# A transformer trunk in split float32: stationary tiles in low SBUF, four seven-product chunks, an accumulating DMA for half of a split

## The chip, the cores and the metric

One core of one Trainium2 chip runs the whole program in one launch. The time is device microseconds of that core. Three runs of the kernel before gave a median of 2034.09 us (2033.9 to 2034.6).

## The reference, cut to what matters

Four layers; each adds half a feed-forward block (FFN), then one attention (differential, block, sparse, differential), then half a second FFN. Inputs, outputs and weights are float32, with 256 tokens of width 1024 and a hidden width of 2816.

```
def swiglu(x, w_in, w_out):
    gate, up = jnp.split(x @ w_in, 2, axis=-1)
    return (jax.nn.silu(gate) * up) @ w_out

for i in range(DEPTH):
    g = norm_g[i]
    h = h + 0.5 * rms_norm(swiglu(rms_norm(h, g[0]), ffn_w_in[i, 0], ffn_w_out[i, 0]), g[1])
    h = h + rms_norm(attention_i(rms_norm(h, g[2])), g[3])
    h = h + 0.5 * rms_norm(swiglu(rms_norm(h, g[4]), ffn_w_in[i, 1], ffn_w_out[i, 1]), g[5])
```

So there are eight FFNs and four attentions. The change touches the FFNs, and in the attentions only the place of some tiles.

## The kernel before, in words

**Split products.** TensorE multiplies in the type fp32r. For float32 accuracy each operand is held as two fp32r tiles, `hi` (a cast) and `lo` (the value less `hi`), and each product is three matmuls: stationary `xh` with moving `hi`, `xh` with `lo`, `xl` with `hi` (`product`, L139 to 151). A matmul has a 128x128 stationary tile (activations, transposed) and a 128x512 moving tile (weights). The activations' tiles are `xh`/`xl` (normed input), `gh`/`gl` (the gated hidden values, transposed in `turn`, L428), `oh`/`ol` (attention output), and `sh`/`sl_` (sums of activations, `sums`, L266).

**Weights.** Weights arrive in blocks of 1 MB as `raw` tiles, loaded by DMAs that SP issues. For each block ACT writes `hi` (`hilo`, L154) and DVE writes `lo` (L155). Four such pairs (UNITS) may be alive; the pool `wt` holds them. Seven raw tiles (RAWS) may be alive. `plan_plain`, `plan_out` and `plan_wino` list the loads and the splits in order, and `fill` (L400) issues them as places come free. A place comes free when TensorE has read a pair for the last time (`close`).

**One FFN.** The hidden width is cut into five chunks of 512 columns (j = 0 to 4) and one of 256. A chunk makes gate and up for two token tiles (t = 0, 1) of 128 tokens. In a plain chunk these are 8 half products (2 token tiles, gate and up, 2 halves of the width 1024) of 12 matmuls each. In a Winograd chunk (`wino`, L465; j = 2 and 4) they are seven such products, named after their weights: `b00`, `t1`, `b10`, `t3`, `t2`, `b11`, `t4`. The weights t1 to t4 are sums of quarters of the weight block, which DVE adds in the raw tiles (L376); the activations' sums are `sh`/`sl_`. The seven results are put together from four PSUM tiles (`pa` to `pd`) with copies on ACT (L483, L488) and adds on DVE (L478). Between these products the chunk also carries the second half of the chunk before it: two transposes (`turn`, PSUM tile `tpg`) and four output steps `o(t, k)` (`out_steps`, L234), each 12 matmuls into the `y` banks with the second weights. Those arrive as two blocks `ko0` and `ko1`.

**Order.** The Tile framework schedules instructions on each engine from the program and its pools' dependencies; so the order on an engine is not that of the code. Pools also set the addresses: a pool is laid out after the one before it. Before, the order in SBUF is `const`, `raw`, `wt`, `xp`, then the work tiles and the pools of the phase. In KiB of each partition: `hi` at 50 to 82, `lo` at 82 to 114, `xh`/`xl` at 114 to 130, `oh`/`ol` at 169 to 185, `sh`/`sl_` at 193 to 209, `gh`/`gl` at 209 to 217.

**The FFN's end** (L554 to 567): after the last chunk's products come its transposes and the last output steps; `turn(last, 1)` stands after `out(last - 1, 1, ...)`.

Of the kernel before, what the change touches and what calls it, by code (L numbers as in the profile page):

```python
# [9 lines left out]
F32 = mybir.dt.float32  # L10
# [6 lines left out]
P = 128  # L17
# [19 lines left out]

RAWS = 7
UNITS = 4
WINO = (2, 4)  # L40

# [5 lines left out]
class Trunk:  # L47
# [217 lines left out]

    def sums(self, X, pool, name):  # L266


        v = self.nc.vector
        half = [[X[t][2][:, b * 512:b * 512 + 512] for b in range(2)] for t in range(NT)]  # L270
        (a00, a01), (a10, a11) = half
        v.tensor_tensor(a11, a11, a10, op=ALU.subtract)
        v.tensor_tensor(a10, a00, a10, op=ALU.subtract)
        v.scalar_tensor_tensor(a00, a11, -1.0, a00, op0=ALU.mult, op1=ALU.subtract)
        v.scalar_tensor_tensor(a01, a01, -1.0, a00, op0=ALU.mult, op1=ALU.subtract)
        out = []
        for t in range(NT):
            sh = pool.tile([P, KD, P], F32R, tag="sh", name=f"sh{name}_{t}")
            sl = pool.tile([P, KD, P], F32R, tag="sl_", name=f"sl_{name}_{t}")
            src = X[t][2].rearrange("p (k n) -> p k n", n=P)  # L280
            self.hilo(src, sh, sl)
            out.append((sh, sl))
        return out

    def ffn(self, l, f, X, ahead, end):
        nc = self.nc
        with self.tc.tile_pool(name=f"ffn{l}{f}", bufs=2, reuse_waits="tile") as pool:
# [36 lines left out]

            def split(n, of, done=False):
# [6 lines left out]
                for k in range(0, nk, m):  # L332
                    self.hilo(v[:, k:k + m], hi[:, k:k + m], lo[:, k:k + m])
                if done:
                    free(of)
                U[n] = hi, lo, nk, w
# [4 lines left out]

            def plan(n, src):
                loads.append(lambda: raw(n, src))
                preps.append((None, lambda: split(n, n, True)))

# [9 lines left out]
            def plan_out(j):  # L355
                c0, w = chunks[j]
                for k in range(0, w // P, 2):
                    plan((j, "o", k), (w_out, c0 + k * P, 2, 0, D))

            def plan_wino(j):  # L360


                c0, w = chunks[j]
                name = lambda n: (j, n)
                quarter = lambda k, u: (w_in, k * 512, 4, u * D_FF + c0, w)
                ko = [(j - 1, "o", k) for k in (0, 2)]
                c1 = chunks[j - 1][0]
                osrc = [(w_out, c1 + k * P, 2, 0, D) for k in (0, 2)]
                for n, src in ((name("b00"), quarter(0, 0)), (name("b01"), quarter(0, 1)),
                               (name("b10"), quarter(1, 0)), (ko[0], osrc[0]), (name("b11"), quarter(1, 1)),  # L370
                               (ko[1], osrc[1])):
                    loads.append(lambda n=n, src=src: raw(n, src))

                def add(to, b):
                    to, b = R[name(to)], R[name(b)]
                    nc.vector.tensor_tensor(to, to, b, op=ALU.add)  # L376

                def t1():
                    add("b00", "b01")
                    split(name("t1"), name("b00"))  # L380

                def t3():
                    add("b01", "b11")
                    split(name("t3"), name("b01"), True)

                def t2():
                    add("b00", "b11")
                    split(name("t2"), name("b00"))

                def t4():  # L390
                    split(name("t4"), name("b00"), True)
                    free(name("b10"))

                mine = [lambda: split(name("b00"), name("b00")), t1, lambda: split(name("b10"), name("b10")),
                        lambda: split(ko[0], ko[0], True), t3, t2]
                mine += [lambda: (add("b00", "b10"), split(name("b11"), name("b11"), True)),
                         lambda: split(ko[1], ko[1], True), t4]
                preps.extend((None, f) for f in mine)

            def fill():  # L400
                while loads and live["raw"] < RAWS:
                    loads.pop(0)()
                while preps and live["unit"] < UNITS:
                    preps.pop(0)[1]()
                    while loads and live["raw"] < RAWS:
                        loads.pop(0)()
# [20 lines left out]
            def turn(j, t):  # L427
# [3 lines left out]
                for k in range(n):  # L431
                    nc.tensor.transpose(tp[:, k, :], g[:, k * P:(k + 1) * P], self.ident)  # L432
                gh = pool.tile([P, 4, P], F32R, tag="gh", name=f"gh{l}{f}_{j}_{t}")
                gl = pool.tile([P, 4, P], F32R, tag="gl", name=f"gl{l}{f}_{j}_{t}")
                self.hilo(tp[:, :n], gh[:, :n], gl[:, :n])
# [30 lines left out]
            def wino(j):  # L466
# [9 lines left out]

                two = lambda name: pool.tile([P, 512], F32, tag=name, name=f"{name}{l}{f}_{j}", bufs=1)
                add = lambda d, x, z: nc.vector.tensor_tensor(d, x, z, op=ALU.add)  # L478
                s24, s31 = SUMS
                p1, p5, u2 = two("p1"), two("p5"), two("u2")  # L480
                A = bank("pa")
                times(A, X[0][0], 0, "b00", True, True)
                nc.scalar.copy(p1, A)  # L483
                fill()
                turn(j - 1, 0)
                B = bank("pb")
                times(B, s31, 4, "t1", True, True)
                nc.scalar.copy(p5, B)  # L488
                fill()
                turn(j - 1, 1)  # L490
                times(A, X[0][0], 4, "b10", False, True)
                sl0 = gate(0, A, 512, j)
# [4 lines left out]
                fill()  # L497
                o(1, 0)
                E = bank("pd")
                times(E, s24, 0, "t2", True, True)  # L500
                add(u2, E, p1)
                add(p5, p5, u2)
                g1 = pool.tile([P, 512], F32, tag="g", name=f"g{l}{f}_{j}_1")
                add(g1, C, p5)
                fill()
                times(B, s24, 4, "b11", False, True)
                g0 = pool.tile([P, 512], F32, tag="g", name=f"g{l}{f}_{j}_0")
                add(g0, B, u2)
                up(0, g0, 512, sl0, j, nr[0], g0)
                fill()  # L510
                o(0, 2)
                times(C, X[1][0], 4, "t4", False, True)
                sl1 = pool.tile([P, 512], F32, tag="sl", name=f"sl{l}{f}_{j}_1")
                add(sl1, C, u2)
                nc.scalar.activation(sl1, sl1, AF.Silu, scale=X[1][1])
# [18 lines left out]
            def early():  # L534
                SUMS.extend(self.sums(X, pool, f"{l}{f}"))
                for t in range(NT):
# [39 lines left out]
    def attention(self, l, _, X, ahead, end):  # L576
        kind, j = l % 3, l // 3
        with self.tc.tile_pool(name=f"attn{l}", bufs=2, reuse_waits="tile") as pool:
# [4 lines left out]
            for t in range(NT):  # L583
                oh = pool.tile([P, KD, P], F32R, name=f"oh{l}_{t}", bufs=1)
                ol = pool.tile([P, KD, P], F32R, name=f"ol{l}_{t}", bufs=1)
                self.oT.append((oh, ol))
# [739 lines left out]
```

## Time and profile before

| What | Value |
|---|---|
| Median of three runs | 2034.09 us |
| The profiled execution's own time | 2035.73 us |
| Its span, first to last instruction | 2034.0 us |
| Mean granted TensorE clock in it (1.0 is full speed) | 0.998 |
| DVE busy | 1575.7 us (77%) |
| ACT busy | 1150.3 us (57%) |
| POOL busy | 135.0 us (7%) |
| Moved by DMA | 363.15 MB, mean 179 GB/s |

The profile is of one execution, 1.6 us longer than the median. The time outside the span is 1.7 us. Busy times of engines overlap, and a matmul's own duration (some 390 ns) overlaps that of the next, so the pace of TensorE is read from the starts of its matmuls, not from their durations. The same holds on ACT and DVE, where an instruction starts a little before the one before it ends.

### The profile page before, as it was taken

How to read it: one execution, taken by the hardware profiler on the slowest of the kernel's cores; microseconds unless marked ns; L12 is line 12 of the kernel's file. 1: busy time of each engine (PE TensorE's matmuls, PEld its weight loads, DVE VectorE, ACT ScalarE, POOL GpSimd, SP SyncE). 2: the span in 40 equal slices, each digit the busy share in tenths (PEclk: the TensorE clock that was granted, in tenths of full speed). 3: DMA queues.
4: the chain of work that ended last, by engine and by line, in shares of the span. 5: the costliest groups of instructions: out<-in, count | busy, mean ns of one | idle time of the engine just before them, and what ended most of it. 6: DMA issues, size and time to landing. Idle time of an engine off the chain costs nothing.

```text
span 2034.0 us, 25675 instructions
## 1 busy us (share of the span) xinstructions
PE 1987.8 (98%) x9904; PEld 1627.4 (80%) x9904; DVE 1575.7 (77%) x2047; ACT 1150.3 (57%) x1581; POOL 135.0 (7%) x239
## 2 busy tenths in 40 slices
PE   8999999999999999999999998999999999999998
PEld 6888777888888878788888877678887888777887
DVE  6877768877888767788787788868777977767875
ACT  6555566555555566455554565755456555566553
POOL 0000210000000110000000032000000000210000
PEclk9999999999999999999999999999999999999999
DMA  9534637544763553663655475145547534537531
GB/s 352 208 134 149 206 104 270 196 135 164 248 226 106 174 179 138 234 223 108 238 176 207 157 178 166 49 176 176 207 151 263 198 133 149 206 104 260 201 130 62
DMA packets 168651, 363.15 MB, mean 179 GB/s; under 512 B 7760, under 2 KB 36688, under 8 KB 168528
## 3 DMA queue, kind: packets, MB, share of 16 engines
q1 hardware_dynamic: 168528, 361.51, 51.7%
q8 instruction: 78, 1.28, 0.3%
q14 instruction: 45, 0.37, 0.1%
HBM read 360.43 MB, written 1.05 MB: 178 GB/s over the span
## 4 chain that ended last, share of the span: by engine, by line
PE 88%; DVE 6%; ACT 3%; issue 2%; POOL 1%; DMA 0%; SPq 0%; POOLq 0%; DVEq 0%; ACTq 0%
PE ps L150 29%; PE y L245 9%; PE y L247 9%; PE y L246 9%; PE pb L150 4%; PE pc L150 4%; PE pa L150 4%; PE pw L665 4%; PE pw L666 4%; PE pw L667 4%; PE pd L150 2%; DVE lo L155 2%; PE tpg L432 2%; PE sc L739 1%; PE tpp L764 1%
## 5 line engine op out<-in xcount | busy, mean ns | idle before, releaser
L155 DVE TENSOR_TENSOR lo<-raw,hi 128x2048 fp32r<-128x2048 f32 (+3 forms) x458 | 875.4, 1924 | 265.3 <-ACT hi L154 264.8
L154 ACT CAST hi<-raw 128x2048 fp32r<-128x2048 f32 (+3 forms) x458 | 731.6, 1609 | 529.6 <-PE ps L150 157.7
L150 PE MATMUL ps<-hi,xh 128*128 128x512 f32 (+1 forms) x1024 | 378.5, 370 | 4.2 <-ACT xh L154 2.4
L150 PE MATMUL ps<-lo,xh 128*128 128x512 f32 (+1 forms) x1024 | 373.8, 365 | 3.9 <-DVE lo L155 2.2
L150 PE MATMUL ps<-hi,xl 128*128 128x512 f32 (+1 forms) x1024 | 372.9, 365 | 0.6 <-DVE st L202 0.6
L245 PE MATMUL y<-hi,gh 128*128 128x512 f32 x704 | 279.5, 397 | 9.5 <-ACT gh L154 9.5
L246 PE MATMUL y<-lo,gh 128*128 128x512 f32 x704 | 277.7, 394 | 0.0
L247 PE MATMUL y<-hi,gl 128*128 128x512 f32 x704 | 277.3, 395 | 0.0
L150 PEld LDWEIGHTS ps<-lo,xh 128*128 128x128 f32 x1024 | 194.5, 190 | 36.0 <-DVE lo L155 6.0
L150 PEld LDWEIGHTS ps<-hi,xh 128*128 128x128 f32 x1024 | 194.3, 190 | 36.1 <-ACT xh L154 4.4
L150 PEld LDWEIGHTS ps<-hi,xl 128*128 128x128 f32 x1024 | 194.2, 190 | 32.7 <-DVE st L202 1.4
L245 PEld LDWEIGHTS y<-hi,gh 128*128 128x128 f32 x704 | 132.6, 188 | 41.8 <-ACT gh L154 13.0
L665 PE MATMUL pw<-hi,xh 128*128 128x512 f32 (+2 forms) x432 | 165.6, 383 | 0.0
L247 PEld LDWEIGHTS y<-hi,gl 128*128 128x128 f32 x704 | 132.6, 188 | 33.0 <-DVE gl L155 2.2
L117 POOL TENSOR_TENSOR st<-st,negh 128x1 f32<-128x1 f32 (+1 forms) x56 | 46.1, 824 | 1682.3 <-DVE st L204 1610.9
L666 PE MATMUL pw<-lo,xh 128*128 128x512 f32 (+2 forms) x432 | 156.7, 363 | 0.0
L667 PE MATMUL pw<-hi,xl 128*128 128x512 f32 (+2 forms) x432 | 156.3, 362 | 0.0
L246 PEld LDWEIGHTS y<-lo,gh 128*128 128x128 f32 x704 | 132.7, 188 | 29.4
L376 DVE TENSOR_TENSOR raw<-raw,raw 128x2048 f32<-128x2048 f32 x64 | 146.4, 2287 | 1.1
L665 PEld LDWEIGHTS pw<-hi,xh 128*128 128x128 f32 x432 | 82.1, 190 | 19.2 <-issue 7.7
L155 DVE TENSOR_TENSOR gl<-tpg,gh 128x512 fp32r<-128x512 f32 (+1 forms) x96 | 61.6, 641 | 45.5 <-ACT gh L154 45.5
L750 ACT ACTIVATE e<-e,st 128x128 f32<-128x128 f32 (+1 forms) x160 | 71.8, 451 | 40.5 <-DVE st L747 39.8
(214 smaller groups left out, 2751.8 us busy)
## 6 DMA issues: line engine op xcount, KB each, us to landing
raw<-in_ffn_w_in SPq DMA_DIRECT2D x172, 1024.0 KB, 5.3
raw<-in_ffn_w_out SPq DMA_DIRECT2D x88, 1024.0 KB, 4.9
raw<-in_diff_w_in SPq DMA_DIRECT2D x24, 1024.0 KB, 5.2
raw<-in_moba_w_in SPq DMA_DIRECT2D x12, 1024.0 KB, 5.4
raw<-in_nsa_w_in SPq DMA_DIRECT2D x9, 1024.0 KB, 5.1
raw<-in_diff_w_out SPq DMA_DIRECT2D x8, 1024.0 KB, 4.8
gpre<-in_norm_g SPq DMA_DIRECT2D x12, 512.0 KB, 6.3
gpost<-in_norm_g SPq DMA_DIRECT2D x12, 512.0 KB, 7.9
```

The lines of the kernel that those rows point to most:

```text
L117: self.nc.gpsimd.tensor_tensor(r, v, src, op=ALU.pow)
L150: nc.tensor.matmul(out, l, r, start=first and i == 0, stop=last and i == len(steps) - 1, skip_group_check=more)
L154: self.nc.scalar.copy(hi, src)
L155: self.nc.vector.tensor_tensor(lo, src, hi.bitcast(F32), op=ALU.subtract)
L245: nc.tensor.matmul(y[b], x[0][:, kt, :], hi[:, k, s], start=f, stop=False)
L246: nc.tensor.matmul(y[b], x[0][:, kt, :], lo[:, k, s], start=False, stop=False)
L247: nc.tensor.matmul(y[b], x[1][:, kt, :], hi[:, k, s], start=False, stop=l)
L376: nc.vector.tensor_tensor(to, to, b, op=ALU.add)
L665: nc.tensor.matmul(out, x[0][:, kt, :], hi[:, k, :], start=first and i == 0, stop=False)
L666: nc.tensor.matmul(out, x[0][:, kt, :], lo[:, k, :], start=False, stop=False)
L667: nc.tensor.matmul(out, x[1][:, kt, :], hi[:, k, :], start=False, stop=last and i == len(todo) - 1)
L750: nc.scalar.activation(e[:, c, :], e[:, c, :], AF.Exp, scale=-1.0, bias=top[:, c:c + 1], accum_out=tot[:, c:c + 1])
```

## The change

1. The pools' order: `wt` and `xp` first, then a new pool `st` (four tiles, for `sh`/`sl_` and for the attention's `oh`/`ol`), a new pool `gt` (`gh`/`gl`, three of each), then `raw`, `const` and the rest. In KiB: `hi` 4 to 36, `lo` 36 to 68, `xh`/`xl` 68 to 84, `st` 84 to 100, `gt` 100 to 112. The scratch for DMAs whose descriptors POOL makes goes from 16384 to 4096 bytes.
2. Four Winograd chunks (j = 1 to 4) in place of two, and eight raw tiles in place of seven, with `t2` in a tile of its own.
3. For `ko0` and `ko1` of those chunks ACT casts `hi`; ACT then writes the negated value, rounded in the same way, into `lo`; a DMA issued by POOL adds the raw value onto it in SBUF, which leaves `lo` = raw less `hi`. DVE has no part in it. The raw tile and `lo` are both bound to that DMA until it has landed.
4. The products come in the order b00, b10, t2, t1, t3, b11, t4. One PSUM tile `pb` gathers b00, t2, t1 and b11 in turn and is copied out between them, so that three adds on DVE replace five.
5. `turn(last, 1)` moves ahead of `ahead()` at the FFN's end.

The diff, cut to its core:

```diff
-RAWS = 7
+RAWS = 8
 UNITS = 4
-WINO = (2, 4)
+WINO = (1, 2, 3, 4)
...
-        self.const = pool("const", 1)
-        self.raw = pool("raw", 3)
         self.wt = pool("wt", UNITS)
         self.xp = pool("xp", 2)
+        self.st = pool("st", 4)
+        self.gt = pool("gt", 3)
+        self.raw = pool("raw", 3)
+        self.const = pool("const", 1)
...
-            sh = pool.tile([P, KD, P], F32R, tag="sh", name=f"sh{name}_{t}")
-            sl = pool.tile([P, KD, P], F32R, tag="sl_", name=f"sl_{name}_{t}")
+            sh, sl = [self.st.tile([P, KD, P], F32R, tag="s", name=f"s{b}{name}_{t}") for b in "hl"]
...
+                if by_dma:
+                    nc.scalar.copy(hi, v)
+                    nc.scalar.activation(lo, v, AF.Copy, scale=-1.0)
+                    nc.gpsimd.dma_start(lo, v.bitcast(F32R), accum_op=ALU.add)
+                else:
+                    for k in range(0, nk, m):
+                        self.hilo(v[:, k:k + m], hi[:, k:k + m], lo[:, k:k + m])
...
+                preps.extend([
+                    lambda: quarters("b00", [("b00", "b00", "b01")]),
+                    lambda: split(ko[0], ko[0], True, True),
+                    lambda: quarters("b10", [("b01", "b01", "b11"), ("t2", "b00", "b11")]),
+                    lambda: split(name("t2"), name("t2")),
+                    lambda: last_of("t1", "b00"),
+                    lambda: last_of("t3", "b01"),
+                    lambda: split(ko[1], ko[1], True, True),
+                    lambda: last_of("b11", "b11"),
+                    lambda: last_of("t4", "t2", ("t2", "t2", "b10"), "b10")])
...
+                B = bank("pb")
+                times(B, X[0][0], 0, "b00", True, True)
+                sl0 = tile("sl", 0)
+                nc.scalar.copy(sl0, B)
                 fill()
                 turn(j - 1, 0)
+                A = bank("pa")
+                times(A, X[0][0], 4, "b10", True, True)
+                add(sl0, A)
+                nc.scalar.activation(sl0, sl0, AF.Silu, scale=X[0][1])
                 fill()
                 turn(j - 1, 1)
+                times(B, s24, 0, "t2", False, True)
+                sl1 = tile("sl", 1)
+                nc.scalar.copy(sl1, B)
                 fill()
                 o(0, 0)
+                times(B, s31, 4, "t1", False, True)
+                g1 = tile("g", 1)
+                nc.scalar.copy(g1, B)
+                fill()
+                o(1, 0)
                 C = bank("pc")
                 times(C, s31, 0, "t3", True, True)
+                add(g1, C)
                 fill()
                 times(B, s24, 4, "b11", False, True)
+                up(0, B, 512, sl0, j, nr[0])
                 fill()
                 o(0, 2)
                 times(C, X[1][0], 4, "t4", False, True)
+                add(sl1, C)
...
             turn(last, 0)
+            turn(last, 1)
             ahead()
...
-            turn(last, 1)
             turn_x()
...
+    nc = bacc.Bacc("TRN2", target_bir_lowering=False, num_devices=1,
+                   dynamic_dma_scratch_size=4096)
```

In the rows that follow, a row gives the line, the operation, and out<-in by the programs' names with their numbers, as the scheduler ordered them. A tile `hi451` is the unit 451; names of a chunk end in FFN, chunk and token tile (`gh01_2_0`: layer 0, second FFN, chunk 2, tile 0).

**ACT, before:** chunk 2 (Winograd) of the second FFN, from the silu of tile 0. The casts are of b11 (419), ko1 (422), t4 (424) and the two blocks after them.

```order
L418 ACTIVATE sl01_2_0_3322<-pa414_3252,st348_2754 128x512
L154 CAST hi419_3325<-raw398_3038 128x2048
L154 CAST hi422_3356<-raw402_3107 128x2048
L154 CAST hi424_3374<-raw382_2873 128x2048
L154 CAST hi428_3399<-raw404_3113 128x2048
L154 CAST hi430_3420<-raw413_3247 128x2048
```

**ACT, after the change:** the same place of chunk 3 of that FFN, from the cast of t3 (447). Units: ko1 449, b11 451, t4 453, the next chunk's b00 457 and ko0 458.

```order
L156 CAST hi447_3558<-raw426_3310 128x2048
L335 ACTIVATE lo449_3588<-raw435_3420 128x2048
L500 COPY sl01_3_1_3585<-pb443_3513 128x512
L334 CAST hi449_3587<-raw435_3420 128x2048
L156 CAST hi451_3620<-raw429_3340 128x2048
L505 COPY g01_3_1_3618<-pb443_3513 128x512
L156 CAST hi453_3638<-raw433_3402 128x2048
L156 CAST hi457_3660<-raw436_3422 128x2048
L334 CAST hi458_3679<-raw440_3462 128x2048
L335 ACTIVATE lo458_3680<-raw440_3462 128x2048
```

Each Winograd chunk has two more writes of 2048 columns on ACT (L335), and the negated one stands ahead of the cast of `hi` for ko1.

**DVE, after the change:** the start of chunk 3 of the second FFN: `lo` of b10 (441), the sum for t2, `gl` of both token tiles around the first add, `lo` of t2 (442). The tile raw433 lies where ko0's raw tile lay.

```order
L157 TENSOR_TENSOR lo441_3492<-raw431_3370,hi441_3491 128x2048
L381 TENSOR_TENSOR raw433_3402<-raw417_3200,raw429_3340 128x2048
L157 TENSOR_TENSOR gl01_2_0_3540<-tpg01_2_0_3534,gh01_2_0_3539 128x512
L484 TENSOR_TENSOR sl01_3_0_3526<-pa446_3543,sl01_3_0_3526 128x512
L157 TENSOR_TENSOR gl01_2_1_3570<-tpg01_2_1_3564,gh01_2_1_3569 128x512
L157 TENSOR_TENSOR lo442_3510<-raw433_3402,hi442_3509 128x2048
```

The sum for t2 writes a tile that the accumulating DMA of ko0 reads, and both `gl` stand behind it.

**PE, after the change:** the same chunk, where b11 (451, into pb443) meets the first output steps with ko1 (449).

```order
L152 MATMUL pb443_3513<-hi451_3620,sh01_0_3016 128x512
L247 MATMUL y411_0_0_3146<-hi449_3587,gh01_2_0_3539 128x512
L248 MATMUL y411_0_0_3146<-lo449_3588,gh01_2_0_3539 128x512
L249 MATMUL y411_0_0_3146<-hi449_3587,gl01_2_0_3540 128x512
L247 MATMUL y411_0_1_3147<-hi449_3587,gh01_2_0_3539 128x512
L248 MATMUL y411_0_1_3147<-lo449_3588,gh01_2_0_3539 128x512
L152 MATMUL pb443_3513<-lo451_3621,sh01_0_3016 128x512
```

Five output matmuls stand inside b11's product; the second of them reads the `lo` that the DMA of ko1 completes, and the rest of b11 stands behind it.

## Rows read from the trace of the kernel before

**Rows 1.** The page, busy time of each engine

```profile
PE 1987.8 (98%) x9904; PEld 1627.4 (80%) x9904; DVE 1575.7 (77%) x2047; ACT 1150.3 (57%) x1581; POOL 135.0 (7%) x239
```

**Rows 2.** The page, chain that ended last, share by engine

```profile
PE 88%; DVE 6%; ACT 3%; issue 2%; POOL 1%; DMA 0%; SPq 0%; POOLq 0%; DVEq 0%; ACTq 0%
```

**Rows 3.** Windows: chunks 2, 3, 4, second FFN; busy PE, PEld, DVE, ACT, POOL, clock, DMA, GB/s

```profile
375.13:406.54 31.41, 31.41 (x142) 25.62 (x141) 27.61 (x19) 19.71 (x14) 0.00 (x0) 1.00 0.72 249
406.54:440.45 33.91, 33.91 (x154) 27.85 (x153) 23.48 (x15) 14.42 (x11) 0.00 (x0) 1.00 0.42 142
440.45:471.86 31.41, 31.41 (x143) 25.62 (x142) 27.59 (x19) 19.71 (x14) 0.00 (x0) 1.00 0.39 134
```

**Rows 4.** The chain of waits in chunk 2: start us, us, what

```profile
375.13 2.73 PE pa L150 x12
...
381.09 0.44 PE tpg L432 x4
...
387.10 2.79 PE pc L150 x12
...
395.46 2.79 PE pb L150 x12
398.26 0.23 PE y L245
...
403.82 2.72 PE pc L150 x12
```

**Rows 5.** Groups of instructions by form, whole span: busy us, mean ns, idle before

```profile
L155 DVE TENSOR_TENSOR lo<-raw,hi 128x2048 fp32r<-128x2048 f32 x308 | 703.0, 2289 | 217.8 <-ACT hi L154 217.7
L376 DVE TENSOR_TENSOR raw<-raw,raw 128x2048 f32<-128x2048 f32 x64 | 146.4, 2287 | 1.1
L245 PE MATMUL y<-hi,gh 128*128 128x512 f32 x704 | 279.5, 397 | 9.5 <-ACT gh L154 9.5
L245 PE MATMUL y<-hi,oh 128*128 128x512 f32 x128 | 52.5, 410 | 0.0
L150 PE MATMUL pb<-hi,sh 128*128 128x512 f32 x128 | 51.8, 405 | 0.0
L150 PE MATMUL pd<-hi,sh 128*128 128x512 f32 x64 | 25.3, 395 | 0.0
L150 PE MATMUL pc<-hi,sh 128*128 128x512 f32 x64 | 25.3, 395 | 0.0
```

**Rows 6.** Timeline of ACT in chunk 2: start us, us, what

```profile
377.90 0.59 ACT L483 COPY p<-pa 128x512 f32<-128x512 f32 x1 [0.78 <-PE pa L150]
378.38 1.90 ACT L154 CAST hi<-raw 128x2048 fp32r<-128x2048 f32 x1
380.19 0.59 ACT L154 CAST gh<-tpg 128x512 fp32r<-128x512 f32 x1
```

**Rows 7.** Timeline of DVE in chunk 2

```profile
385.77 0.68 DVE L155 TENSOR_TENSOR gl<-tpg,gh 128x512 fp32r<-128x512 f32 x1
386.37 2.28 DVE L376 TENSOR_TENSOR raw<-raw,raw 128x2048 f32<-128x2048 f32 x1
388.57 2.28 DVE L155 TENSOR_TENSOR lo<-raw,hi 128x2048 fp32r<-128x2048 f32 x1
```

**Rows 8.** Timeline of PE at the second FFN's end

```profile
501.31 0.50 PE L245 MATMUL y<-hi,gh 128*128 128x512 f32 x1 [1.78 <-ACT gh L154]
```

**Rows 9.** The page: DMA queue (packets, MB, share); loads, median us to landing

```profile
q1 hardware_dynamic: 168528, 361.51, 51.7%
...
raw<-in_ffn_w_out SPq DMA_DIRECT2D x88, 1024.0 KB, 4.9
```

**Rows 10.** DMA in chunk 2 of the second FFN, loads: median us to landing

```profile
raw<-in_ffn_w_in SPq DMA_DIRECT2D x6, 1024.0 KB, 7.2
raw<-in_ffn_w_out SPq DMA_DIRECT2D x2, 1024.0 KB, 6.3
```

**Rows 11.** POOL's most frequent group, whole span

```profile
L117 POOL TENSOR_TENSOR st<-st,negh 128x1 f32<-128x1 f32 x48 | 38.0, 792 | 1618.4 <-DVE st L204 1610.9 <-DVE st L538 7.2
```

More of the change, by code (lines that the diff above doesn't have):

```diff
@@ L262, in ybanks, with sums @@
         return [(self.ya, self.yb)[t].tile([P, 512], F32, tag="y", name=f"y{self.n}_{t}_{b}") for b in range(2)]
-    def sums(self, X, pool, name):
+    def sums(self, X, name):
         v = self.nc.vector
@@ L331, in split @@
                 v = R[of][:, :nk * w].rearrange("p (k n) -> p k n", n=w)
-                for k in range(0, nk, m):
-                    self.hilo(v[:, k:k + m], hi[:, k:k + m], lo[:, k:k + m])
+                if by_dma:
[5 more added lines that the diff above has]
+                        self.hilo(v[:, k:k + m], hi[:, k:k + m], lo[:, k:k + m])
                 if done:
@@ L340, in close, with plan @@
                 live["unit"] -= 1
-            def plan(n, src):
+            def plan(n, src, by_dma=False):
                 loads.append(lambda: raw(n, src))
-                preps.append((None, lambda: split(n, n, True)))
+                preps.append(lambda: split(n, n, True, by_dma))
             def plan_plain(j):
@@ L357, in plan_out @@
                 for k in range(0, w // P, 2):
-                    plan((j, "o", k), (w_out, c0 + k * P, 2, 0, D))
+                    plan((j, "o", k), (w_out, c0 + k * P, 2, 0, D), j < last - 1)
             def plan_wino(j):
@@ L368, in plan_wino @@
                 osrc = [(w_out, c1 + k * P, 2, 0, D) for k in (0, 2)]
-                for n, src in ((name("b00"), quarter(0, 0)), (name("b01"), quarter(0, 1)),
-                               (name("b10"), quarter(1, 0)), (ko[0], osrc[0]), (name("b11"), quarter(1, 1)),
+                for n, src in ((name("b00"), quarter(0, 0)), (ko[0], osrc[0]), (name("b01"), quarter(0, 1)),
+                               (name("b11"), quarter(1, 1)), (name("b10"), quarter(1, 0)), (name("t2"), None),
                                (ko[1], osrc[1])):
@@ L372, in plan_wino @@
                     loads.append(lambda n=n, src=src: raw(n, src))
[L374 to L398, printed above, removed]
+                def add(to, a, b):
+                    nc.vector.tensor_tensor(R[name(to)], R[name(a)], R[name(b)], op=ALU.add)
@@ new lines, in quarters, with last_of @@
+                def quarters(n, then=()):
+                    split(name(n), name(n))
+                    for x in then:
+                        add(*x)
+                def last_of(n, of, before=None, gone=None):
+                    if before:
+                        add(*before)
+                    if gone:
+                        free(name(gone))
+                    split(name(n), name(of), True)
+                preps.extend([
[8 more added lines that the diff above has]
+                    lambda: last_of("t4", "t2", ("t2", "t2", "b10"), "b10")])
@@ L432, in turn @@
                     nc.tensor.transpose(tp[:, k, :], g[:, k * P:(k + 1) * P], self.ident)
-                gh = pool.tile([P, 4, P], F32R, tag="gh", name=f"gh{l}{f}_{j}_{t}")
-                gl = pool.tile([P, 4, P], F32R, tag="gl", name=f"gl{l}{f}_{j}_{t}")
+                gh = self.gt.tile([P, 4, P], F32R, tag="gh", name=f"gh{l}{f}_{j}_{t}")
+                gl = self.gt.tile([P, 4, P], F32R, tag="gl", name=f"gl{l}{f}_{j}_{t}")
                 self.hilo(tp[:, :n], gh[:, :n], gl[:, :n])
@@ L512, in wino @@
                 times(C, X[1][0], 4, "t4", False, True)
-                sl1 = pool.tile([P, 512], F32, tag="sl", name=f"sl{l}{f}_{j}_1")
-                add(sl1, C, u2)
+                add(sl1, C)
                 nc.scalar.activation(sl1, sl1, AF.Silu, scale=X[1][1])
@@ L534, in early @@
             def early():
[L535 removed]
+                SUMS.extend(self.sums(X, f"{l}{f}"))
                 for t in range(NT):
@@ L583, in attention @@
             for t in range(NT):
-                oh = pool.tile([P, KD, P], F32R, name=f"oh{l}_{t}", bufs=1)
-                ol = pool.tile([P, KD, P], F32R, name=f"ol{l}_{t}", bufs=1)
+                oh, ol = [self.st.tile([P, KD, P], F32R, tag="s", name=f"o{b}{l}_{t}") for b in "hl"]
                 self.oT.append((oh, ol))
```

29 lines of the change are left out of this document (4 added, 25 removed).

## The prediction, made before the changed kernel ran

> **What bounds the kernel now.** I read the busy times first, and TensorE leads: PE is busy 98% of the span [rows 1]. The chain that ended last agrees, 88% of it on PE, 6% on DVE, 3% on ACT, 0% on DMA [rows 2]. So a chunk costs what its matmuls cost, unless something is late. The windows of three chunks of one FFN show this: PE is busy for all of each, 31.41 us in both Winograd chunks, 33.91 us in the plain one between them, at full clock, with DVE busy for 27.6 us of the 31.41 [rows 3]. That leaves DVE 3.8 us, so nothing can be added to DVE freely. Last I read the chain inside a Winograd chunk for the pace. Twelve matmuls with stationary `xh` or `xl` take 2.73 and 2.72 us, some 227 ns each; twelve with `sh` take 2.79 us, and the 24 output matmuls with `gh`/`gl` from 398.26 to 403.82 take 231.7 ns each [rows 4]. The moving tile has the same shape in all of them, so some 5.5 ns (taken from starts of matmuls over the whole trace, which lie at 226 to 227 and 232 ns) go with where the stationary tile lies, or with what it is.
>
> **Part A: two more chunks of seven products.** Two chunks in each of eight FFNs change from eight products of 12 matmuls to seven: 2 x 8 x 12 = 192 matmuls fewer. At 0.227 us that is 43.6 us. The check: 33.91 less 31.41 is 2.50 us [rows 3], near 12 x 0.227 = 2.72 less 0.26 for 48 matmuls with `sh` at 5.5 ns more each.
>
> **Part B: the stationary tiles' place.** The slow products are those whose stationary tiles lie high in SBUF; `xh`/`xl` lie lowest. After the change all lie below 112 KiB, beside the weights. The forms are `gh` 704, `oh` 128, and `sh` 128, 64 and 64 [rows 5], each with its `lo` and its low stationary partner: 3 x 1088 = 3264 matmuls. At 5.5 ns, if the place is the reason, 18.0 us. The other bound is 0, if it is something else about these tiles. The rows show only that the two go together; I take the full sum since three different tiles from three pools share one pace.
> The Trainium skill, "TensorE: Matmul & The Clock Gate", section "Step-by-step: what each phase is for", speaks against this part: it says TensorE reads moving and stationary operands through two independent ports, so that loading the next stationary tile takes nothing from the running matmul. It has no dependence on an address, and by it the part gives 0. The rows' 2.72 against 2.79 us show a difference that it does not name.
>
> **Part C: the FFN's end.** The output matmul there waits 1.78 us for the cast of `gh` [rows 8]; over the program this form idles 9.5 us, all for `gh` [rows 5]. With `turn(last, 1)` earlier, six other output blocks stand between cast and reader. Gain 9.5 us. What comes next there, the transposes of x for the next phase, is needed only after twelve more matmuls (2.7 us).
>
> **Part D: what the chunk now has to meet.** I walked the new order of one steady chunk by hand, each engine with the durations of the rows, started apart as they are on it: ACT's cast 1.81 us and copy 0.48 [rows 6], DVE's wide operation 2.20 and narrow 0.60 [rows 7], PE's twelve 2.73 and a transposing block 0.44 [rows 4]. PE's own work is 132 x 0.2275 + 2 x 0.44 = 30.9 us.
> DVE has 11 wide operations, five narrow adds or `gl`, and two products of 0.66: 28.5 us. It fits, and its slack falls to 2.4 us. Without the DMAs it would have 13 wide ones, 32.9 us, and would be the bound: what the accumulating DMAs hide is 4.4 us of DVE. ACT's two more writes fit into its 11 us of idle time. In the walk PE waits 0.1 us in all, if `lo` is in time.
> That rests on X, the time from POOL's issue to landing. For ko1 ACT's negated write must wait until TensorE has read t2's `lo` (13.05 us after the chunk's start; four pairs are alive), ends at 14.95, and PE reads the sum at 20.5: X may be 5.5 us, and beyond that TensorE waits one for one, with the rest of b11 behind it. For ko0, issued 3.2 us before the chunk starts, DVE's sum for t2 is the first that waits, at 3.83: X may be 7.1; behind it stand both `gl`, which TensorE needs for `o(0, 0)`. SP's loads too wait for a raw tile that an accumulate still holds; they run a chunk ahead, and I count nothing. If that lead were gone they would cost X one for one.
> No row shows an accumulating DMA. From below: a plain load of the same 1 MB lands 4.9 us after issue [rows 9]. From above: an accumulate also reads its destination. The queue's 51.7% of the span for 361.51 MB [rows 9] makes 2.9 us of all engines for 1 MB, so 4.9 + 2.9 = 7.8; and where loads crowd, they take 6.3 to 7.2 us [rows 10], 1.4 to 2 more. POOL's own preparation may add some 0.8 us, its price of a small instruction [rows 11]. I take 6.0: nearest the plain transfer, with POOL's 0.8 and 0.3 for sharing, on the assumption that second read and write overlap. Nothing shows that they do; it is the weakest term. Then ko1 is 0.5 us late per chunk. I add 0.1 from the walk and 0.3 for hand-offs that it can't see. Over 32 chunks D costs 32 x 0.9 = 28.8 us.
> The Trainium skill, "DMA: Bandwidth & Descriptors", section "Anatomy of one DMA — SWDGE (gpsimd) path", gives 2.0 us plus bytes over 436 kB per us: as an estimate 4.4 us here, and no term for an accumulate; no run here shows such a DMA. By it, ko1 would be in time, and the sum some 16 us lower.
>
> **The rest.** The narrow adds fall from five to three per Winograd chunk and are in DVE's 28.5. The eighth raw tile and the single PSUM tile cost no time by themselves; the copies between the products are ACT's 0.48 us, hidden by transposes or output blocks. If such a cover were gone, each would cost 0.5 us, 1.0 to 1.5 a chunk (rival 2). Placing `raw` and `const` higher I price at nothing: DVE's and ACT's rows show one duration for all.
>
> **Sum.** Against the profiled execution's 2035.7 us: 2035.7 - 43.6 - 18.0 - 9.5 + 28.8 = 1993.4. The median lies 1.6 lower: 1992 us.
>
> **Rivals.**
> 1. The accumulates land late, and the kernel gets **slower**. With A to C at 71.1 us, the point is a wait of 71.1 / 32 = 2.2 us per chunk. At X = 7.2 ko1 alone costs 1.7, ko0 0.1, and 0.4 goes to the rest: that is the point. With X = 7.8 ko1 costs 2.3, ko0 0.7, and 0.4 more: 32 x 3.4 = 109 us, so 2035.7 - 71.1 + 109 - 1.6 = 2072 us. For it: the second read, and loads that crowd [rows 10]. Against: DMA stands at 0% of the chain [rows 2], and its share falls to 0.4 in two of three chunks [rows 3]. Chance 0.23, with some of it beyond 2072.
> 2. DVE or a hand-off becomes the bound: DVE's slack of 2.4 us is one wide operation, and a chunk slips by 1 us more: 1992 + 32 = 2024. For it: DVE's 28.5 of 30.9. Against: the walk. Chance 0.11.
> 3. The place does nothing (B = 0): 2010. Speaking for it is that only a correlation is shown; against it, three tiles with one pace. Chance 0.08.
> 4. `lo` is always in time and no hand-off slips: X near 4.9, D = 0.1 x 32 = 3.2: 1966. Chance 0.06.
> 5. Gains and waits cancel (2030 to 2038): X about 7.2. Chance 0.06.
> The forecast, 1975 to 2005, has 0.46.
>
> **How the numbers follow.** About 0.2% (4 us) is what a measurement of this kernel can tell from no change. Forecast and rivals 2, 3 and 4 are faster: 0.71. Rival 5 is the same: 0.06. Rival 1 is slower: 0.23. The range runs from 1966 (rival 4) to 2050 (X about 7.4), and leaves out some 0.18 above and 0.02 below. The forecast's own range is 1975 to 2005.
>
> **What would show each step.** A: 192 fewer wide matmuls, four chunks alike near 31 to 32 us. B: `y`, `pb` and `pc` blocks at 227 ns instead of 232. C: no wait of `y` for `gh` at an FFN's end. D: the time from POOL's issue to landing on the DMA list, and PE's waits for `lo` in the output block within b11 and in `o(0, 0)`. If X is above 7 us there, rival 1 holds; if PE waits for `lo` that DVE writes or for casts, rival 2. It is wrong if PE waits by more than 2.2 us per Winograd chunk, wherever.

## The result: 14% slower

The changed kernel took 2323.22 us (median of four runs, 2321.91 to 2327.83), the kernel before 2033.99 us: a ratio of 1.1426, with a 95% interval of 1.1406 to 1.1446. The forecast was 1992 us, with a range that ended at 2050. The profiled execution took 2327.83 us, at a mean granted clock of 0.941 in place of 0.998.

These lines of the changed kernel's page answer to [rows 1, 2, 9]: busy time of each engine, the chain that ended last, two DMA queues, and the time from issue to landing.

```profile
PE 2036.0 (88%) x9712; PEld 1638.7 (70%) x9712; DVE 1686.7 (73%) x2111; ACT 1376.4 (59%) x1757; POOL 198.6 (9%) x303
...
PE 53%; DMA 21%; issue 11%; ACT 7%; DVE 6%; POOL 1%; POOLq 0%; SPq 0%; ACTq 0%; DVEq 0%
...
q1 hardware_dynamic: 168528, 361.51, 45.4%
q0 software_dynamic: 9216, 67.11, 14.1%
...
raw<-in_ffn_w_out SPq DMA_DIRECT2D x88, 1024.0 KB, 6.5
lo<-raw POOLq DMA_DIRECT2D x64, 1024.0 KB, 10.5
```

PE's busy share falls from 98% to 88% though it has 192 instructions fewer, and DMA, which had 0% of the chain, has 21%. The new queue q0 holds the 64 accumulating DMAs. They take 14.1% of the engines' span, so 0.141 x 2326 / 64 = 5.1 us of all 16 engines for one block (1024 KB, or 1.05 of the page's MB), while a load of one block takes 0.454 x 2326 / 361.51 x 1.05 = 3.1 us. Their median time to landing is 10.5 us; the forecast was worked out with 6.0.

The groups of instructions (busy us, mean ns, idle before and its cause) show who waits:

```profile
L248 PE MATMUL y<-lo,gh 128*128 128x512 f32 x704 | 293.2, 420 | 240.1 <-DMA lo<-raw 240.0
...
L381 DVE TENSOR_TENSOR raw<-raw,raw 128x2048 f32<-128x2048 f32 x128 | 292.3, 2284 | 21.0 <-DMA lo<-raw 17.1
```

And so do PE's waits (total us, times, the longest):

```profile
PE y L248 <- DMA lo<-raw: 240.0, 42, 8.2
PE tpx L181 <- DVE xg L225: 14.6, 11, 2.5
```

The output matmul that reads `lo` waits 240 us for the DMA, 42 times; DVE's sums wait 17 us for it. The wait for `xg` is read below.

**One steady chunk.** A window of one chunk's length in the second FFN (busy PE, PEld, DVE, ACT, POOL, then clock, DMA share, GB/s), beside [rows 3]:

```profile
426.30:467.20 40.90, 33.66 (x138) 26.38 (x136) 28.90 (x18) 23.41 (x18) 1.71 (x2) 0.92 0.69 205
```

It takes 40.90 us where the walk had 30.9 of work and 0.9 of waits. The chain of waits there, in order of time (start, us, what):

```profile
438.20 0.39 ACT sl L500
438.59 12.55 DMA lo<-raw
451.14 0.04 issue
451.18 0.80 PE y L248
451.98 0.43 PE y L249
...
453.26 3.90 PE pb L152 x11
...
458.77 2.72 PE pc L152 x12
```

Once ACT has written the negated value, POOL issues ko1's DMA at 438.59, and it lands 12.55 us later. PE's timeline has the wait that this makes (start, duration, and in brackets the idle time before it):

```profile
451.18 0.80 PE L248 MATMUL y<-lo,gh 128*128 128x512 f32 x1 [7.05 <-DMA lo<-raw]
```

PE does its next matmuls at 0.43 us each in place of 0.23; eleven of b11 take 3.90 us, some 355 ns each. The same stretch cut into four windows, with the columns of the window above:

```profile
438.20:444.10 5.90, 5.90 (x25) 4.54 (x25) 3.80 (x2) 5.90 (x6) 0.85 (x1) 1.00 1.02 316
444.10:451.18 7.08, 0.03 (x1) 0.00 (x0) 5.60 (x4) 2.36 (x2) 0.00 (x0) 0.86 1.01 270
451.18:457.16 5.98, 5.98 (x16) 4.72 (x17) 0.00 (x0) 0.00 (x0) 0.00 (x0) 0.59 0.88 321
457.16:464.21 7.05, 7.05 (x32) 5.82 (x32) 5.63 (x4) 6.26 (x4) 0.85 (x1) 1.00 0.82 261
```

PE works at full clock until 444.1, then does 0.03 us in 7.08 us. The granted clock falls to 0.86 in that stretch and is 0.59 in the next, mostly the lower of its two levels (1.2 of 2.4 GHz), where 16 matmuls take 5.98 us and not 16 x 0.227 = 3.6. After that it is 1.00 again. So this wait of 7.0 us costs 9.4. With the walk's 30.9 that makes 40.3 of the 40.9 us. DMA's share is 1.0 through the wait: its engines are full.

POOL's timeline has the two issues of this chunk, first ko0's, then ko1's:

```profile
419.59 0.85 POOL L336 DMA_DIRECT2D lo<-raw  x1 [20.04 <-ACT lo L335]
438.59 0.85 POOL L336 DMA_DIRECT2D lo<-raw  x1 [18.15 <-ACT lo L335]
```

The DMA view of the window from 419.5 to 427 us holds one transfer, ko0's:

```profile
lo<-raw POOLq DMA_DIRECT2D x1, 1024.0 KB, 7.5
```

The same view from 432 to 442 us, where ko1's is issued among three loads:

```profile
raw<-in_ffn_w_in SPq DMA_DIRECT2D x3, 1024.0 KB, 9.9
lo<-raw POOLq DMA_DIRECT2D x1, 1024.0 KB, 12.6
```

Same bytes, same path: 7.5 us nearly alone, 12.6 us among loads that themselves take 9.9. Over all 64 (min, median, max):

```profile
DMA to landing us min/median/max: 6.9/10.5/13.3
```

Taken apart in order of issue, the 32 of ko0 have a median of 7.0 us and the 32 of ko1 one of 12.25. DVE's load does not explain the difference: the DMA issued at 378.01 met no load, DVE was busy all the while it ran, and it landed in 7.0 us. So the first theory was: ko1's DMA is late because loads crowd it; an accumulate has a second read; and the clock adds to each wait.

### The profile page after: what moved, and what is told of

Its sections match the earlier page's. It is cut to its first block, busy times and chain, and to the rows that moved or that the text cites. A ratio compares the mean times of both kernels' runs of the same rounds, so it can differ in the third digit from the quotient of the medians.

```text
span 2326.1 us, 25710 instructions
## 1 busy us (share of the span) xinstructions
PE 2036.0 (88%) x9712; PEld 1638.7 (70%) x9712; DVE 1686.7 (73%) x2111; ACT 1376.4 (59%) x1757; POOL 198.6 (9%) x303
## 3 DMA queue, kind: packets, MB, share of 16 engines
q1 hardware_dynamic: 168528, 361.51, 45.4%
q0 software_dynamic: 9216, 67.11, 14.1%
HBM read 360.43 MB, written 1.05 MB: 155 GB/s over the span
## 4 chain that ended last, share of the span: by engine, by line
PE 53%; DMA 21%; issue 11%; ACT 7%; DVE 6%; POOL 1%; POOLq 0%; SPq 0%; ACTq 0%; DVEq 0%
DMA lo<-raw 20%; PE pb L152 10%; PE ps L152 7%; PE y L248 7%; PE y L249 5%; PE y L247 5%; PE pw L667 3%; PE pw L668 3%; PE pw L669 3%; PE pa L152 3%; PE pc L152 3%; DVE lo L157 2%; ACT lo L335 2%; ACT hi L156 2%; PE sc L741 1%
## 5 line engine op out<-in xcount | busy, mean ns | idle before, releaser
L157 DVE TENSOR_TENSOR lo<-raw,hi 128x2048 fp32r<-128x2048 f32 (+2 forms) x442 | 832.2, 1909 | 162.5 <-ACT hi L156 161.1
L156 ACT CAST hi<-raw 128x2048 fp32r<-128x2048 f32 (+2 forms) x442 | 693.4, 1597 | 287.3 <-PE pb L152 83.7
L381 DVE TENSOR_TENSOR raw<-raw,raw 128x2048 f32<-128x2048 f32 x128 | 292.3, 2284 | 21.0 <-DMA lo<-raw 17.1
L152 PE MATMUL ps<-hi,xh 128*128 128x256 f32 (+1 forms) x512 | 176.7, 345 | 1.3 <-ACT xh L156 1.3
L152 PE MATMUL ps<-hi,xl 128*128 128x256 f32 (+1 forms) x512 | 175.1, 342 | 0.5 <-DVE st L204 0.5
L152 PE MATMUL pb<-lo,sh 128*128 128x512 f32 x384 | 172.9, 450 | 2.4 <-DVE lo L157 2.4
L152 PE MATMUL ps<-lo,xh 128*128 128x256 f32 (+1 forms) x512 | 174.4, 341 | 0.0
L152 PE MATMUL pb<-hi,sh 128*128 128x512 f32 x384 | 169.1, 440 | 0.0
L152 PE MATMUL pb<-hi,sl 128*128 128x512 f32 x384 | 168.5, 439 | 0.0
L247 PEld LDWEIGHTS y<-hi,gh 128*128 128x128 f32 x704 | 135.9, 194 | 39.0 <-ACT gh L156 12.6
L335 ACT ACTIVATE lo<-raw 128x2048 fp32r<-128x2048 f32 x64 | 122.6, 1916 | 45.8 <-PE pb L152 44.6
## 6 DMA issues: line engine op xcount, KB each, us to landing
lo<-raw POOLq DMA_DIRECT2D x64, 1024.0 KB, 10.5
```

The source lines that it names most:

```text
L152: nc.tensor.matmul(out, l, r, start=first and i == 0, stop=last and i == len(steps) - 1, skip_group_check=more)
L156: self.nc.scalar.copy(hi, src)
L157: self.nc.vector.tensor_tensor(lo, src, hi.bitcast(F32), op=ALU.subtract)
L247: nc.tensor.matmul(y[b], x[0][:, kt, :], hi[:, k, s], start=f, stop=False)
L335: nc.scalar.activation(lo, v, AF.Copy, scale=-1.0)
L381: nc.vector.tensor_tensor(R[name(to)], R[name(a)], R[name(b)], op=ALU.add)
```

## The experiments

All times are medians; the ratio is to the kernel before, on the same chip, with its 95% interval.

### Only ko0's lo by DMA

```diff
-                    lambda: split(ko[1], ko[1], True, True),
+                    lambda: split(ko[1], ko[1], True),
```

> Edit: only ko0's lo comes by the accumulating DMA; ko1's is subtracted on DVE. Theory (crowding at ko1): the loss is ko1's DMA, which shares the engines with three loads and takes 12 us where ko0's takes 7 us alone. So PE's wait of y for lo by DMA falls from 240 us to under 20, the granted clock is back above 0.99, DVE has 12 wide operations in a chunk (30.7 of 30.9 us), a chunk takes 31 to 32.5 us: 1980 to 2015 us. Rival 1 (any accumulating DMA costs the chunk some 7 us, wherever it is): waits for ko0's lo stay and the time is above 2150. Rival 2 (DVE becomes the bound): chunks of 33 us and more, waits for lo by DVE, 2040 to 2080.

Measured: 2105.21 us, 1.0345 (1.0313 to 1.0377). PE's waits for the DMA:

```profile
PE y L248 <- DMA lo<-raw: 53.4, 25, 5.4
```

and of where its accumulating DMAs landed:

```profile
DMA to landing us min/median/max: 6.9/8.4/10.6
```

Most of the loss goes with ko1's DMA: 218 us of 289. But the theory promised 1980 to 2015 and under 20 us of such waits, and ko0's DMA no longer lands in 7.0 us: its median is 8.4. In the trace up to three loads are in flight beside it, where in the changed kernel it mostly met one at its end or none. So ko0's quiet place was not fixed by the schedule; it seems to have come with the long waits. The other 71 us over the kernel before were not taken apart: besides the DMA, PE waits 15.6 us for `gl` and 6.7 us for `gh`, and DVE, with 12 wide operations, is at work for 31 to 33 us of a chunk.

### ko1 split earlier

```diff
                     lambda: last_of("t1", "b00"),
-                    lambda: last_of("t3", "b01"),
                     lambda: split(ko[1], ko[1], True, True),
+                    lambda: last_of("t3", "b01"),
```

> Edit: ko1's split stands ahead of t3's in the list of splits, so that ko1 takes the pair that b10 leaves and t3 the one that t2 leaves. Theory (crowding and lateness): its DMA is issued some 4 us earlier in the chunk, mostly ahead of the loads, lands in 7 to 10 us, and PE has some 10 us to cover it: waits under 2 us a chunk, 1985 to 2040 us. Rival 1 (the loads move with it and crowd it as before, 12 us): 2 to 3 us of wait a chunk, 2050 to 2090 with the clock. Rival 2 (t3 becomes late instead): no waits for lo by DMA, but 2 to 4 us of waits for lo of t3 by DVE, 2040 to 2100.

Measured: 2118.59 us, 1.0400 (1.0382 to 1.0417), above the ranges of the theory and of both rivals. The DMAs land after a median of 10.9 us: ko1's still takes 10.2, and ko0's, 7.0 before, now takes 11.1. So the crowd did not go away, as rival 1 says; it now meets both. Waits for the DMA itself fall to 38.8 us. A window of 41 us in the same FFN, somewhat more than a chunk:

```profile
426.00:467.00 41.00, 37.13 (x155) 30.09 (x154) 33.02 (x22) 26.06 (x20) 1.71 (x2) 0.92 0.76 217
```

DMA's share is 0.76 and DVE has 33.0 us of 41: both are higher than in the changed kernel's window, and neither is full. What makes up the time beyond the waits for the DMA is not shown.

### Both lo on DVE

```diff
-                    lambda: split(ko[0], ko[0], True, True),
+                    lambda: split(ko[0], ko[0], True),
...
-                    lambda: split(ko[1], ko[1], True, True),
+                    lambda: split(ko[1], ko[1], True),
```

> Edit: no accumulating DMA; both lo are subtracted on DVE, all else as changed. Theory (the DMA is the whole loss, and DVE is what it was to relieve): no wait for a DMA, clock near 1, DVE's 13 wide operations make 32.9 us a chunk, so 2 to 3 us of PE's time: 2027 to 2060 us. Rival (the new order of products and the one PSUM tile cost by themselves): chunks above 35 us and a time above 2100.

Measured: 2076.24 us, 1.0203 (1.0188 to 1.0218), 16 us over the theory's range and under the rival's. Two Winograd chunks in windows:

```profile
382.70:417.76 35.06, 32.48 (x142) 25.18 (x141) 34.38 (x22) 20.63 (x17) 0.00 (x0) 1.00 0.48 173
417.76:452.48 34.72, 32.38 (x142) 25.31 (x141) 34.54 (x22) 22.13 (x17) 0.00 (x0) 1.00 0.53 188
```

DVE is busy 34.4 of 35.06 us and 34.5 of 34.72; PE has 2.6 and 2.3 us of idle time and the clock is full. The chunks are bound by DVE, at 34.7 to 35.1 us, where 13 wide operations had been put at 32.9. That is more than the 33.91 us of the plain chunk that they replace [rows 3]. No accumulating DMA is left here, and the kernel is still slower than before: with both `lo` on DVE, four Winograd chunks gain nothing. That both `lo` would have to leave DVE is not shown; one `lo` on DVE was run only beside the crowded DMA, in the first experiment.

### A plain copy in place of the accumulate

```diff
-                    nc.gpsimd.dma_start(lo, v.bitcast(F32R), accum_op=ALU.add)
+                    nc.gpsimd.dma_start(lo, v.bitcast(F32R))
```

The tile `lo` then holds the raw value instead of the rest.

> Edit: the two DMAs on POOL copy the raw value over lo instead of adding it (lo is then the raw value, so the products are other ones; same instructions, same bytes written). Theory A (the second read of the accumulate costs time): issue to landing falls from 7.0 to about 5 us alone and from 12 to about 8 to 9 crowded, PE waits 3 us a chunk instead of 7: 2080 to 2200 us. Theory B (only the crowd and POOL's path cost): 7 and 12 us stay, and the time stays within 10 us of 2323.

Measured: 2205.15 us (one run), 5 us above theory A's range and 118 below theory B's figure. In the DMA view, ko0's transfer of one chunk, issued at 433.45, which met the end of one load only:

```profile
lo<-raw POOLq DMA_DIRECT2D x1, 1024.0 KB, 4.3
```

and ko1's of that chunk, issued at 451.92, which did:

```profile
lo<-raw POOLq DMA_DIRECT2D x1, 1024.0 KB, 9.1
```

Over all, 4.3 us in the quiet places and 9.4 in the crowded ones (medians of ko0's and ko1's), against 7.0 and 12.25. So the accumulate costs 2.7 to 2.9 us more than a copy, and the crowd 5.1 to 5.3, with either. The queue's row on the page says where the 2.7 come from:

```profile
q0 software_dynamic: 9216, 67.11, 7.7%
```

A copy takes 0.077 x 2203 / 64 = 2.65 us of all 16 engines, the accumulate 5.1, nearly twice as much. Theory A holds for the second read and is not the whole: a copy that reads nothing twice would still be 3.9 us late beside the 5.5 us that ko1 has.
The Trainium skill, "DMA: Bandwidth & Descriptors", section "Anatomy of one DMA — SWDGE (gpsimd) path", gives 4.4 us for these bytes as an estimate; the quiet copy's 4.3 agrees. That fit has no term for accumulating and none for sharing, and those are the 8 us between its estimate and ko1's 12.25.

### The loads held until ko1's DMA has landed

```diff
-                while loads and live["raw"] < RAWS:
+                while loads and live["raw"] < RAWS and not hold:
...
-                    lambda: split(name("t2"), name("t2")),
+                    lambda: (split(name("t2"), name("t2")), hold.append(1)),
...
-                    lambda: split(ko[1], ko[1], True, True),
+                    lambda: (split(ko[1], ko[1], True, True), quiet(ko[1]), hold.clear()),
...
+                    if late:
+                        nc.sync.dma_start(r[:, :1], late.pop()[:, 0, :1].bitcast(F32))
```

`quiet` puts ko1's `lo` twice into the list `late`.

> Edit on the changed kernel: the loads that are issued around ko1's accumulating DMA (three of 1 MB) are held until it has landed; two of them get a small DMA out of ko1's lo into their tile first, so that they wait. Theory (the crowd makes 12 us out of 7): ko1's DMA lands in 7 to 8 us, PE waits for it 1 to 2.5 us a chunk instead of 7, and the time falls below 2200 us, unless the held loads come late in their turn (then the waits for lo by DMA still fall to under 80 us, and others by loads appear). Rival (ko1's DMA is slow for another reason: its place, its issue): it stays at 11 to 13 us, waits for it above 200 us.

Measured: 2227.02 us, 1.0942 (1.0919 to 1.0965), not the 2200 and less that the theory asked for. Now ko1's DMA, issued at 434.30, lands soonest:

```profile
lo<-raw POOLq DMA_DIRECT2D x1, 1024.0 KB, 8.0
```

while ko0's of the next chunk, issued at 449.66, stands among the loads that were held (the window from 441 to 456 us):

```profile
raw<-in_ffn_w_in SPq DMA_DIRECT2D x3, 1024.0 KB, 14.8
raw<-in_ffn_w_out SPq DMA_DIRECT2D x2, 1024.0 KB, 12.4
lo<-raw POOLq DMA_DIRECT2D x1, 1024.0 KB, 11.2
```

The two have changed places: 8.0 us for ko1, 11.2 for ko0. That is what the crowd as the cause asks for, and a reason that lies in ko1's own place or issue does not give it. PE's waits for the DMA halve, to 116 us, not under 80 as expected: the held loads only moved the crowd. A chunk loads six blocks, 6 x 3.1 us of all engines, and accumulates two, 2 x 5.1: 28.6 us, the 0.69 to 0.71 of 40.9 us that the windows show. In a chunk of 31 us it would be 92%. By this sum such a chunk has no quiet place for two of these DMAs. A chunk with fewer bytes to load was not tried.

### Two halves

```diff
-                    nc.scalar.activation(lo, v, AF.Copy, scale=-1.0)
-                    nc.gpsimd.dma_start(lo, v.bitcast(F32R), accum_op=ALU.add)
+                    for k in range(nk):
+                        nc.scalar.activation(lo[:, k], v[:, k], AF.Copy, scale=-1.0)
+                        nc.gpsimd.dma_start(lo[:, k], v[:, k].bitcast(F32R), accum_op=ALU.add)
```

> Edit on the changed kernel: the negated write and the accumulating DMA in two halves of 512 KB, so that the output steps' first half waits for the first half alone. Theory (bytes in the queues beside the loads set the time): the first half of ko1 lands in 6 to 9 us and is issued 0.9 us earlier, PE waits 2 to 4 us a chunk: 2130 to 2230 us. Rival (queueing behind whole loads, whatever the own size): both halves land in 11 to 13 us and the time stays above 2290.

Measured: 2272.79 us, 1.1175 (1.1152 to 1.1197), between the two. The halves still take a median of 9.3 us for half the bytes, and ko1's first half one of 9.2, just above the theory's 6 to 9. PE's waits:

```profile
PE y L248 <- DMA lo<-raw: 110.4, 43, 5.2
PE y L249 <- DVE gl L157: 65.1, 18, 4.8
```

The direct wait falls from 240 to 110 us, and 65 us turn up behind DVE's `gl`, which stand behind the sum for t2; DVE idles 67 us before its sums.

### POOL subtracts

```diff
-                    nc.scalar.activation(lo, v, AF.Copy, scale=-1.0)
-                    nc.gpsimd.dma_start(lo, v.bitcast(F32R), accum_op=ALU.add)
+                    nc.gpsimd.tensor_tensor(lo, v, hi.bitcast(F32), op=ALU.subtract)
```

> Edit on the changed kernel: POOL subtracts lo = raw - hi for ko0 and ko1 itself, with no second write on ACT and no DMA. Theory (the loss is the crowded DMA, nothing else in the chunk): if POOL takes under 6 us for one and leaves DVE's pace alone, waits under 1 us a chunk and 1975 to 2030 us. Rival (POOL slow, or DVE's wide operations slowed beside it): DVE above 2400 ns each or POOL above 8 us, and 2060 to 2250 us.

Measured: 2238.33 us, 1.1000 (1.0978 to 1.1021): the rival. The groups of wide operations on DVE and on POOL:

```profile
L157 DVE TENSOR_TENSOR lo<-raw,hi 128x2048 fp32r<-128x2048 f32 x292 | 739.4, 2557 | 90.5 <-ACT hi L156 90.0
L380 DVE TENSOR_TENSOR raw<-raw,raw 128x2048 f32<-128x2048 f32 x128 | 389.1, 3045 | 0.0
L335 POOL TENSOR_TENSOR lo<-raw,hi 128x2048 fp32r<-128x2048 f32 x64 | 375.6, 5868 | 893.9 <-ACT hi L334 840.5 <-issue 53.4
```

POOL takes 5.9 us for one, and the means of DVE's two wide groups rise from 2289 and 2287 ns [rows 5] to 2557 and 3045. These means hide what happens. Two rows of the timeline:

```profile
433.49 10.73 POOL L335 TENSOR_TENSOR lo<-raw,hi 128x2048 fp32r<-128x2048 f32 x1 [17.59 <-ACT hi L334]
440.38 5.98 DVE L157 TENSOR_TENSOR lo<-raw,hi 128x2048 fp32r<-128x2048 f32 x1
```

POOL's subtraction ends at 444.22, and DVE's, begun before that, at 446.36, 2.14 us later, about its own duration without POOL. The same holds for all 58 of DVE's wide operations that took over 2.5 us in this run: each ends 2.14 to 2.15 us after one on POOL, while those that meet none on POOL take 2.28 us. So DVE's wide operation is not slowed beside POOL's; it waits until POOL's has ended. The reverse seems to hold too: two wide operations of DVE run at 2.2 us each from 435.37 on, inside this subtraction, which takes 10.73 us where POOL's shortest takes 4.7. The 64 on POOL thus take time from DVE, which had none.

### The places alone, and the places with the tail

```diff
-        self.const = pool("const", 1)
-        self.raw = pool("raw", 3)
         self.wt = pool("wt", UNITS)
         self.xp = pool("xp", 2)
+        self.st = pool("st", 4)
+        self.gt = pool("gt", 2)
+        self.raw = pool("raw", 3)
+        self.const = pool("const", 1)
```

with `sh`/`sl_`, `oh`/`ol` and `gh`/`gl` in the new pools; the second also moves `turn(last, 1)` up and has three of each in `gt`.

> Edit on the kernel before: only the pools' order and the two new pools (and the smaller scratch, to make room); same instructions in the same form. Theory (place of the stationary tile sets 227 or 232 ns): 3264 matmuls lose 5.5 ns, 18 us: 2014 to 2019 us. Rival (the 227 ns came with the order of products or with something else in the change): 2032 to 2036 us.

> Edit on the kernel before: the pools' order and turn(last, 1) moved ahead. Theory: the 9.5 us of waits for gh go too, so 2004 to 2010 us, the fastest of all kernels here. Rival (that wait is only moved to the transposes of x behind it): 2013 to 2019 us, as with the pools' order alone.

Measured: 2020.21 us, 0.9932 (0.9918 to 0.9947), and 2017.76 us, 0.9917 (0.9901 to 0.9932). The chain in the places' chunk 2, with stationary `sh`, `sh` and `xh`:

```profile
378.46 2.75 PE pb L152 x12
...
387.12 2.72 PE pc L152 x12
...
403.44 2.75 PE pc L152 x12
```

The blocks with `sh` now take 2.75 and 2.72 us, the one with `xh` 2.75; before, `sh` took 2.79 and `xh` 2.72 or 2.73 [rows 4]. Over the whole trace the median step from one matmul to the next falls from 232 to 227 ns with `gh` and with `sh` and stays at 227 with `xh`. So it is the place. Which property of the place counts, its height in SBUF or its distance to the weights, was not tested. The gain is 14.5 us of the 18.0 that were worked out, and the time lies 1 us above the theory's range. PE's waits with the places alone:

```profile
PE y L247 <- ACT gh L156: 9.5, 8, 1.8
PE tpx L181 <- DVE xg L225: 7.8, 7, 2.2
```

and with the tail:

```profile
PE tpx L181 <- DVE xg L225: 14.4, 9, 2.6
```

The 9.5 us for `gh` go, but the transposes of x now wait for the next input, `xg`, on DVE: none before (but for the program's start), 7.8 us with the places, 14.4 with the tail. With the places these waits stand for others: PE's waits of `ps` for its inputs fall from 8.6 to 1.7 us. With the tail the further 6.6 us take most of the 9.5, as its rival says; the tail's own 2.4 us lie inside the two intervals.

### Two and three Winograd chunks, lo on DVE

```diff
-WINO = (1, 2, 3, 4)
+WINO = (2, 4)
```

with both `lo` on DVE; the second kernel has (1, 2, 4).

> Edit on the changed kernel: Winograd in chunks 2 and 4 alone as before, and both lo on DVE, no DMA on POOL; it keeps the places, the new order of products, the one PSUM tile, eight raw tiles and the tail. Theory (the two chunks between give DVE its slack back): 2008 to 2022 us, near the pools' order with the tail. Rival (the new order of products costs by itself): above 2030.

> Edit on the changed kernel: Winograd in chunks 1, 2 and 4, both lo on DVE. Theory (DVE's wide operations bound consecutive Winograd chunks): 8 x 2.3 us less of PE, and 2 to 3 us of wait in one or two of the chunks of each FFN: 2010 to 2040 us, not below the one with two. Rival (DVE's slack in the plain chunk carries three): 1990 to 2005 us, the fastest.

Measured: 2014.78 us, 0.9904 (0.9887 to 0.9920), the fastest here, though not told apart from the places with the tail; and 2048.59 us, 1.0065 (1.0050 to 1.0080), above the ranges of theory and rival. With two, the new order of products costs nothing that shows, and the output matmuls wait for nothing:

```profile
L247 PE MATMUL y<-hi,gh 128*128 128x512 f32 x704 | 275.8, 392 | 0.0
```

With three, PE waits for DVE's `gl` and ACT's `gh`, 22 us in these two alone:

```profile
PE y L249 <- DVE gl L157: 13.5, 13, 1.5
PE y L247 <- ACT gh L156: 8.9, 16, 0.7
```

and the second of the two consecutive Winograd chunks has DVE at work nearly throughout, as in the kernel with four:

```profile
377.04:412.10 35.06, 32.47 (x142) 25.18 (x141) 34.38 (x22) 20.69 (x17) 0.00 (x0) 1.00 0.51 184
```

So with both `lo` on DVE each further Winograd chunk costs: 34 us for the third and 28 for the fourth in eight FFNs, where 192 / 2 x 0.227 = 21.8 us were to be gained by each.

## Why the prediction was wrong, point by point

- **What fails is part D's X.** "I take 6.0: nearest the plain transfer", with 7.8 as the bound from above and 1.4 to 2 more where loads crowd. Measured: 7.0 alone, 12.25 for ko1. The assumption that "second read and write overlap" is wrong: the accumulate takes 2.7 us more than a copy on the same path, and 5.1 us of all engines against 2.65; the bound from above had added 2.9 (3.05, if a block is counted as 1.05 MB). The crowd was put at 0.3 us, with 1.4 to 2 as its end; it is 5.2. The loads' 6.3 to 7.2 us [rows 10] were read as an end of the range, though ko1's DMA is issued while three loads are on their way. The prediction's own sign of being wrong, over 2.2 us of waits per Winograd chunk, is met: 240 us in 32 chunks are 7.5.
- **Two other parts of D held.** ko0's median of 7.0 us lies within the 7.1 that the walk gives it; DVE's sums wait 17 us for it in all. SP's loads, counted as nothing, do wait for the accumulates (453 us on SP's queue), but ACT and DVE wait 3 us in all for a block of weights.
- **The cover was right.** ko1's DMA is issued at 438.59 and PE wants it at 444.13: 5.5 us, as walked. Beyond it PE waits one for one, 7.05 us where the DMA took 12.55.
- **The clock was not in the sum.** The wait of 7.05 us is followed by work at the lower level that takes 2.4 us more than at the full one, which made each late microsecond there cost a third more. In the trace of before the only wait as long (8.1 us, for `xg`) stands at the program's start, and no price was taken.
- **"Against: DMA stands at 0% of the chain"** was a bad reason. A resource that hides well says nothing of its room. The room could be worked out: six loads at 3.1 us in a chunk of 31 are 60%; two accumulates at two passes of 3.1 would have filled the rest.
- **A** is right in its count (PE 9904 to 9712 instructions) and never shows as time, because the chunk is bound elsewhere. **Rival 2** is true without the DMAs: 34.7 to 35.1 us a chunk.
- **B**: the cause is right, rival 3 falls; 14.5 of 18.0 us, with steps 5 ns shorter and not 5.5. By the two independent ports that the Trainium skill names ("TensorE: Matmul & The Clock Gate", section "Step-by-step: what each phase is for") the part would have given nothing; the runs show 227 against 232 ns by place alone, and the measurement decides.
- **C**: "needed only after twelve more matmuls" named the wrong wait. The transposes' reader was covered; their source, `xg`, was not.
- **Rival 1** named the mechanism and the sign, with 2072 us. At its own formula with X = 12.25 for ko1 the wait is 6.75 us a chunk; with 0.4 and 2.4 for the clock, 32 x 9.55 = 306 us, and 2035.7 - 71.1 + 306 - 1.6 = 2269. The rest, 54 us, is 11 us that B and C did not give, and the first Winograd chunk of each FFN, whose window is some 3 us longer than the others', about 24 us; why those are longer was not taken apart, and some 20 us stay open.

## What to carry to other kernels

Before moving an operation to DMA, add up the DMA engines' time in the stage, not their share over the program and not their place in the chain: each accumulate took 5.1 us of all engines per block where a load took 3.1 and a copy 2.65, and with loads it filled them. Take the time to landing from the moment of issue: ask which loads the same step sets free. A late operand cost its wait here and, behind it, the clock: 2.4 us after 7.0.

## What was not expected of the hardware

The stationary tiles' place in SBUF changed a matmul's pace by 5 ns of 232, with the same instructions. An accumulating DMA within SBUF took 7.0 us alone against 4.3 for a copy. And DVE's wide operations waited for POOL's subtraction to end: all 58 that were held up ended 2.14 to 2.15 us after it.
